# Low halves of the expert weights on one engine, one comparison for eight one-hot tiles, Silu and Tanh instead of Sigmoid

## The chip, the core and the metric

The kernel runs on one core of a Trainium2 chip. The metric is the device time of one execution in microseconds (us); the time given for a kernel is the median of its runs. Five engines work side by side and wait for each other through semaphores: PE (TensorE, matrix products; PEld are its weight loads), DVE (VectorE), ACT (ScalarE), POOL (GpSimd) and SP (SyncE, which here only issues transfers). Each engine works through its own list of instructions in order.

## The reference

One layer of a hybrid encoder over 1024 tokens of width 1024: four mixers side by side, an output projection, then a mixture of 16 experts and a gate. The change touches only the part behind the output projection:

```python
def expert_choice_moe(x, router_w, w_gate, w_up, w_down):
    aff = softmax(x @ router_w)                      # 1024 tokens x 16 experts
    gate, idx = top_k(swapaxes(aff), 128)            # each expert takes 128 tokens
    xs = x[idx]
    h = silu(xs @ w_gate) * (xs @ w_up)              # weights 1024 x 1024, fp32, per expert
    ye = (h @ w_down) * gate
    return zeros.at[idx].add(ye)

h = h + expert_choice_moe(rmsnorm(h, norm_ffn_w), ...)
gate = sigmoid(rmsnorm(h, ple_norm_w) @ ple_gate_w)
h = h + gate * (p @ ple_proj_w)
return rmsnorm(h, final_norm_w)
```

## The kernel before

The first 880 us hold the mixers and the output projection; the change does not touch them. After them `experts` walks through the 16 experts in turn. For each expert three matrices of 1024 x 1024 fp32 numbers are read from HBM, in tiles of 128 x 1024 (512 KB), 24 tiles an expert. `chunk` handles two tiles at a time: a transfer into a buffer `raw` (six of them; for early experts some go ahead of time into `room`), a cast on ACT into the high half `wh` (L1620), and a subtraction raw - wh that gives the low half `wl` (L1622). The subtraction frees the raw buffer, and SP then issues the next transfer into it. `mm3` multiplies in three passes: high x high (L1651), high x low (L1652), low x high (L1653). `up` does this for the gate and up matrices, `down` for the third one.

`spare` decides which engine subtracts. It counts the tiles: from the second expert's worth of tiles on, six of every 24 go to POOL, and from the tenth expert on four of every 24; all others go to DVE. Two tiles of the first expert go to POOL by an argument of their own.

Three more things belong to the change:

- `slot_sums` turns the slot numbers of an expert's tokens into one-hot matrices: eight comparisons of 128 x 128 on DVE (L1926), each followed by a small product (L1927). `pick` uses it for each of the 16 experts, `pick_tile` for each of seven groups of 128 finished tokens.
- `up` ends with silu: ACT computes a sigmoid (L1991), and DVE multiplies twice (L1992 by the gate product, L1993 by the up product).
- `tile_finish` computes the sigmoid gate of a group of finished tokens (from the 11th expert on, a group per expert): a sigmoid on ACT (L2164), a multiplication by the projected embedding `pp` (L2165), an addition (L2166). The group's rows come from HBM by indices, with transfers that POOL issues: `gather` (L1959) from `H` into `a` and from `PP` into `b`. Experts' tokens are gathered from `HN` two experts ahead, and their results are added to `H` by a scatter (L2012).

The instructions' order on each engine is worked out by a scheduler when the kernel is built, from what each one depends on; it is the same in every execution.

Of the kernel before, what the change touches and what calls it, by code (L numbers as in the profile page):

```python
# [25 lines left out]
def host_constants():  # L26
# [32 lines left out]
    # rotary tables  # L59
# [5 lines left out]
    # retention decays  # L65
# [8 lines left out]
    # long-filter features and decay  # L74
# [11 lines left out]
    # 2048-point transform as 16 x 128: cos, sin, -sin of [n2, k1 + 16 k2], and the same transposed  # L86
# [23 lines left out]
def woven(*parts):  # L110
    """emits the steps of several generators side by side, each spread over the whole"""
    work = [[list_len, g, 0] for g, list_len in parts]
    live = set(range(len(work)))
    while live:
        i = min(live, key=lambda k: (work[k][2] + 0.5) / work[k][0])
        try:
            next(work[i][1])
            work[i][2] += 1
            yield
        except StopIteration:  # L120
            live.discard(i)


class Body:
# [19 lines left out]
    @contextmanager  # L144
    def after(self, *ins):
        """what is traced here is queued behind these instructions"""
        with ExitStack() as order:
            for i in ins:
                if i is not None:
                    order.enter_context(self.tc.issue_after(i))  # L150
            yield
# [47 lines left out]
    def rsqrt(self, out, in_, scale, eps):  # L199
        """out = (in * scale + eps) ** -0.5"""  # L200
# [5 lines left out]
    def split_T(self, xn_tiles, half, w_name, hi, lo, tag, bufs):  # L206
        """transposes 4 token tiles [128, 1024] to hi/lo [128, 8, 512*half..], scaled per feature"""
# [55 lines left out]
    def load_w(self, w, segs):  # L263
        """columns of a weight [1024, n] -> (wh, wl) [128, 8, n], w == wh + wl"""
# [25 lines left out]
    def proj_cm(self, c0, evac):  # L290
        """128 channels of w_in, channel-major: evac(half, psum[128, 512]); 8 steps"""
# [15 lines left out]
    def proj_tm(self, segs, evac):  # L307
        """columns of w_in, token-major: evac(t, psum[128, n]); 16 steps"""
# [20 lines left out]
class Gdn:  # L329
    def conv_tile(self, c0, name, taps, ti, ntot, bias=None, half=True):  # L330
        """128 channels projected channel-major and convolved along time -> [128, 1024]"""
# [18 lines left out]
    def silu_half(self, out, acc):  # L350
        """out = silu(2 * acc)"""
# [5 lines left out]
    def softplus(self, out, x, n, tag):  # L357
        """out = log(1 + exp(x)) on [128, n], accurate to float32's rounding beside exp's own"""
# [17 lines left out]
    def bias_rows(self):  # L376
        """per-head constants on every partition"""
# [9 lines left out]
    def gdn_proj(self):  # L387
# [8 lines left out]
        # gates, token-major: z | a | b, and the state-space dt  # L396
# [44 lines left out]
    def swapped(self, ap, rev=False):  # L441
        """halves of each tile swapped, or all tokens of it reversed as well"""
        v = ap.rearrange("p (t b i) -> p t b i", t=8, b=2)
        return v[:, :, ::-1, ::-1] if rev else v[:, :, ::-1, :]
# [13 lines left out]
    def gdn_values(self):  # L458
        """4 steps"""
# [24 lines left out]
    def gdn_rates(self):  # L484
        nc = self.nc
        # [128, (kind dir head), tile]
# [8 lines left out]
        # rhs for the permuting products: g | beta | rk, as [dir, tile, head]  # L495
# [10 lines left out]
        # split of g for the decay sums  # L506
# [6 lines left out]
    def gdn_scalars(self):  # L513
# [10 lines left out]
        # e^{gc}, e^{gl - gc}, e^{gl} (other half), e^{gc} (own token order)  # L524
# [12 lines left out]
        # beta * rk of the column tokens, one row per block  # L537
# [11 lines left out]
    def gdn_prep(self, d, t):  # L549
        """decay, key and query products of one tile and direction; X to the block layout, the scan's matrices"""  # L550
# [42 lines left out]
        # decayed queries, in their own token order  # L593
# [10 lines left out]
        # decay of the state  # L604
# [4 lines left out]
        # token-major k in block order  # L609
# [12 lines left out]
    def gdn_inverse(self):  # L622
        """inverts the diagonal 32 x 32 blocks of every system, one system to a partition"""
        nc = self.nc
        # per row: first block | second block; the upper right blocks
# [3 lines left out]
        # per row: first inverse turned | first inverse | second inverse; products  # L629
# [30 lines left out]
    def gdn_scan(self):  # L660
# [11 lines left out]
        # rows of the upper token block: upper right block | inverse turned | inverse | its product; lower: 0 | inverse  # L672
# [13 lines left out]
        def place(d, s):  # L686
            """token half and state half of a step, and its block"""
# [17 lines left out]
        def invert(d, i, part):  # L705
            """the inverse's upper right block"""
# [17 lines left out]
        def solve(d, i):  # L724
            """the inverse times keys and values; values go under the states, keys into what multiplies the states"""
# [105 lines left out]
    def gdn_preps(self):  # L831
        """16 steps"""
# [8 lines left out]
# rows of a spectrum: k0, k8, then real and imaginary parts of these  # L841
# [7 lines left out]
class Mix:  # L849
    def tokens(self, src, fn, tag, bufs):  # L850
        """[128 channels, 1024 tokens] -> fn(tile slice, psum [128 tokens, 4 tiles, 128 channels])"""
# [8 lines left out]
    # ---- projections and convolutions -> DRAM  # L860
# [73 lines left out]
    # ---- state-space mixer  # L934
    def ssm(self):
# [7 lines left out]
        # a = dt * A, split; [128, dir, tile, head]  # L943
# [20 lines left out]
        def sc(x, t, n=64):  # L964
            """[128, 2, 32] scalars of a tile as [128, 4, 2, n]"""
            return x[:, :, t * 4:t * 4 + 4].rearrange("p d h -> p h d")[:, :, :, None].to_broadcast([128, 4, 2, n])

        # states before and after each tile, both directions; what a tile adds first stands in the next one's place
# [4 lines left out]
        # to what a tile adds, the state of the tile before comes, decayed over that tile  # L973
# [38 lines left out]
        def weights(t):  # L1012
            """decay from each source to each target"""
# [26 lines left out]
        def combine(t, E, pg, py, pi):  # L1040
            # forward and backward parts of the products of B and C, decayed
# [39 lines left out]
    def norm_store(self, y, t, col):  # L1081
        """rmsnorm over 256 columns, to the mixed rows; the norm's weights are in the rows of w_out"""
# [8 lines left out]
    # ---- long convolutions  # L1091
    def hy_mlp(self):
        """hidden layers of the filters' network: positions 512 h + c on the partitions of half h; and 1024 - (512 h + c)"""
# [44 lines left out]
    def hy_transforms(self):  # L1138
        """16-point parts of the transforms of filter and signal, 64 channels at a time -> DRAM; 8 + 8 steps"""
# [4 lines left out]
        # both directions of the filter as one circular one of 2048  # L1144
# [5 lines left out]
        for q in range(4):  # L1150
# [16 lines left out]
            # what passes straight through  # L1167
            nc.gpsimd.tensor_tensor(out=S[0:1, 0, 0], in0=S[0:1, 0, 0], in1=bi, op=OP.add)
            # sums and differences of points half a turn apart
# [16 lines left out]
    def spectrum(self, z, k1, M):  # L1186
        """the points k1 + 16 k2, real and imaginary"""
# [17 lines left out]
    def dft16(self, u, x, z, w):  # L1205
        """sums u and differences x [128, 8, n] of points n and n + 8 of 16 -> rows z(i), as above"""
# [45 lines left out]
    def idft16(self, z, y):  # L1252
        """transpose of dft16: z as above -> y [128, 8, 256]; even points first"""
# [64 lines left out]
    def hy(self):  # L1318
# [4 lines left out]
        def rows(name):  # L1323
            """row i of a spectrum, or n of them"""
# [18 lines left out]
        def forward(k1):  # L1343
# [5 lines left out]
            # product with the filter  # L1349
# [47 lines left out]
    # ---- retention  # L1397
    def ret(self):
        """8 steps for the states, 8 more for the outputs, tiles falling"""
# [8 lines left out]
        def pq2(rev):  # L1408
            """tail and head powers of each head, or head and tail, as [128, 4, 2, 64]"""
# [4 lines left out]
        # states before and after each tile, as in the state-space mixer  # L1414
# [6 lines left out]
        def decayed(d, t, src):  # L1421
            """adds the state of the tile before, decayed over that tile"""
# [49 lines left out]
        def finish(t, r, po):  # L1472
            # group norm over each head
# [10 lines left out]
            # in the place of the state it came from  # L1484
# [12 lines left out]
    def open_stage(self):  # L1497
        """long convolutions and state-space mixer where the projections were"""
# [10 lines left out]
    def open_spare(self):  # L1509
        """what the experts' phase has no room for"""  # L1510
# [30 lines left out]
    def projections(self):  # L1541
        """4 + 12 + 16 + 16 steps"""
# [35 lines left out]
class Ffn:  # L1578
    def pool(self, name, side):
        """a stack with one pool of its own"""  # L1580
# [21 lines left out]
    def chunk(self, w, c, pool=False, behind=(), norm=None, first=0, load_behind=None, load_on=None, raw=None, wh=None,  # L1602
              wl=None):
        """256 rows of a weight [1024, 1024], times a norm's weights -> [(hi, lo), (hi, lo)], [128, 1024] each"""
        nc = self.nc
        out = []
        for k in range(2):
# [6 lines left out]
            with self.after(*behind):  # L1614
# [4 lines left out]
                else:  # L1619
                    nc.scalar.copy(h, r)  # L1620
                    e = nc.gpsimd if pool or self.spare(self.turns) else nc.vector
# [4 lines left out]
    def spare(self, n):  # L1626
        """whether GpSimd takes the n-th conversion"""
        n -= 1
        return n >= 24 and n % 24 in ((3, 7, 11, 15, 19, 23) if n < 24 * FIRST else (0, 10, 17, 20))

    def rows_T(self, x, hi, lo, tag=("sp", 2), head=None):
        """[128 rows, 1024] -> transposed [128, 8, 128] split; the first columns may lie elsewhere"""
# [13 lines left out]
    def mm3(self, ps, xh, xl, k, w, half, first, last):  # L1646
        """three-pass product of one k tile into a 512-column half"""
# [7 lines left out]
    def sumsq_rstd(self, x, s):  # L1655
# [3 lines left out]
        self.on_pool = self.rsqrt(s[:, 1:2], s[:, 0:1], 1.0 / D, EPS)  # L1659

    def out_proj(self):
# [36 lines left out]
        def multiply(t, hi, lo, xt):  # L1698
            """a step before, between and after halves of the second half of the columns"""
# [14 lines left out]
        def route(t, xt):  # L1714
            """the norm's weights are in the router's, its scale comes with the softmax"""
# [11 lines left out]
            # softmax over the experts  # L1727
# [51 lines left out]
    def top_128(self, i, pt):  # L1779
        """takes the i-th tile's weights [16 experts, 128 tokens] into the search of each expert's 128 largest"""  # L1780
        nc = self.nc
        if i == 0:
            # lanes of 32 partitions, each a list of every expert
# [11 lines left out]
        def order(w):  # L1795
            """lists that rise, then fall, or the other way round: to falling ones"""
# [8 lines left out]
        def merge(w, x, out):  # L1805
            """the 128 largest of two falling lists, rising and falling"""
# [4 lines left out]
        # two tiles at a time, as four lists of 64  # L1811
# [32 lines left out]
    def slots_of(self):  # L1844
# [11 lines left out]
        # slots, counted from 1: larger ones first, then equal ones in order of tokens  # L1856
# [17 lines left out]
        # what a slot takes over: token within its tile, tile, gate in three parts  # L1874
# [17 lines left out]
    def ranks(self):  # L1892
        """tokens in order of the last expert that takes them, from 1; the last expert's own have none"""
# [26 lines left out]
    def slot_sums(self, slot, e, n):  # L1920
        """of what an expert's slots take over, n sums for each of the slots numbered from 1 [128, n]"""
# [322 lines left out]
```

## Time and profile before

| | |
|---|---|
| time, median of 3 runs | 1687.73 us (1683.22 to 1689.33) |
| span of the profiled execution | 1691.1 us (no other time of this execution is given) |
| PE busy | 1525.9 us, 90% |
| DVE busy | 1236.0 us, 73% |
| ACT busy | 863.1 us, 51% |
| POOL busy | 773.4 us, 46% |
| DMA | 362.55 MB, mean 214 GB/s |

The span runs from the first to the last instruction, and shares are of that span. Averages over the whole span mix the mixers with the experts, so the rows below are mostly cut by stretch: 880 to 960 us (the routing's end and the first expert), 960 to 1133 us (about four experts), 1133 to 1350 us (about five), 1350 to 1624 us (five, each with a gate group) and the rest. An instruction that waits inside an engine for a port or for operands counts as busy; an engine that waits for a semaphore counts as idle, and the profile says which instruction's end released it.

### The profile page before, as it was taken

Reading aid. Unit: us, or ns where it says so; the run is one execution under the profiler, and the core shown is the slowest. Engines: PE = TensorE matmul, PEld = TensorE weight load, DVE = VectorE, ACT = ScalarE, POOL = GpSimd, SP = SyncE. Lnnn points to the kernel's source line nnn. Section 1 sums busy time; section 2 is a strip of 40 time slices with the busy share of each in tenths; the row PEclk is TensorE's granted clock in tenths of the full one; section 3 lists DMA queues with packets and bytes.
Section 4 is the critical chain, followed back from the end, with each engine's and each line's share of the span. In section 5 each row is a group of like instructions: output and inputs, shape, how many; then the busy total and the mean of one; then the engine's idle time right before and its main releaser. Section 6 shows DMA issues by size and latency. Waiting matters only on the chain.

```text
span 1691.1 us, 26196 instructions
## 1 busy us (share of the span) xinstructions
PE 1525.9 (90%) x9148; PEld 1250.7 (74%) x9148; DVE 1236.0 (73%) x2175; ACT 863.1 (51%) x1413; POOL 773.4 (46%) x856
## 2 busy tenths in 40 slices
PE   4999998999999899689988988889888899889997
PEld 4877778998778767578876766677666688777786
DVE  5589777922546568756777998889888886877773
ACT  6254342133443345332335766677676667656762
POOL 3117665662763368451324344554444443344441
PEclk9999999998999899789989999999999999989998
DMA  5213557363553674263447987789999988877871
GB/s 181 56 37 111 155 175 234 110 182 112 146 145 115 238 236 134 72 203 133 178 149 280 351 318 268 272 301 345 337 335 331 319 292 288 295 274 253 287 276 51
DMA packets 200673, 362.55 MB, mean 214 GB/s; under 512 B 62046, under 2 KB 124732, under 8 KB 200285
## 3 DMA queue, kind: packets, MB, share of 16 engines
q1 hardware_dynamic: 169016, 296.13, 50.8%
q0 software_dynamic: 12400, 42.29, 8.2%
q10 hardware_dynamic: 19125, 22.45, 3.9%
q8 instruction: 72, 1.18, 0.3%
q14 instruction: 60, 0.49, 0.1%
HBM read 301.04 MB, written 59.77 MB: 213 GB/s over the span
## 4 chain that ended last, share of the span: by engine, by line
PE 41%; DVE 19%; DMA 18%; issue 10%; POOL 8%; ACT 5%; SPq 0%; POOLq 0%; ACTq 0%; DVEq 0%
PE pj L300 8%; DVE wl L1622 6%; PE pj L318 5%; PE ga L1652 4%; DMA raw<-in_exp_w_up_dram 4%; PE ga L1653 4%; PE ga L1651 4%; POOL prm L1208 2%; POOL prr L1208 2%; ACT wh L1620 2%; DMA a<-H,tidx 2%; DMA raw<-in_exp_w_gate_dram 2%; PE pj L1652 2%; PE pj L1653 2%; PE pj L1651 2%
## 5 line engine op out<-in xcount | busy, mean ns | idle before, releaser
L1622 DVE TENSOR_TENSOR wl<-raw,wh 128x1024 fp32r<-128x1024 f32 x270 | 388.2, 1464 | 75.1 <-ACT wh L1620 71.6
L1620 ACT CAST wh<-raw 128x1024 fp32r<-128x1024 f32 x344 | 356.4, 1053 | 145.8 <-DMA raw<-in_exp_w_gate_dram 50.2
L1622 POOL TENSOR_TENSOR wl<-raw,wh 128x1024 fp32r<-128x1024 f32 x74 | 195.4, 2642 | 230.8 <-ACT wh L1620 213.9
L1652 PE MATMUL ga<-wl,xh 128*128 128x512 f32 x512 | 210.1, 410 | 27.4 <-DVE wl L1622 15.0
L1653 PE MATMUL ga<-wh,xl 128*128 128x512 f32 x480 | 191.2, 399 | 0.0
L1651 PE MATMUL ga<-wh,xh 128*128 128x512 f32 x480 | 179.2, 409 | 3.6 <-ACT wh L1620 3.1
L1652 PEld LDWEIGHTS ga<-wl,xh 128*128 128x128 f32 x512 | 98.3, 192 | 63.6 <-DVE wl L1622 29.9
L300 PE MATMUL pj<-hnh,wh 128*128 128x512 f32 x288 | 120.1, 417 | 0.8 <-ACT cin L337 0.8
L318 PE MATMUL pj<-wh,hnh 128*128 128x256 f32 (+1 forms) x384 | 112.0, 292 | 9.5 <-DVE zss L915 6.9
L300 PE MATMUL pj<-hnl,wh 128*128 128x512 f32 x288 | 118.5, 411 | 0.0
L300 PE MATMUL pj<-hnh,wl 128*128 128x512 f32 x288 | 118.1, 410 | 0.0
L1652 PE MATMUL pj<-wl,hh 128*128 128x512 f32 x256 | 105.2, 412 | 11.7 <-DVE wl L1622 10.9
L1651 PEld LDWEIGHTS ga<-wh,xh 128*128 128x128 f32 x480 | 91.4, 193 | 26.8 <-ACT wh L1620 7.0
L318 PE MATMUL pj<-wh,hnl 128*128 128x256 f32 (+1 forms) x384 | 110.4, 288 | 0.0
L318 PE MATMUL pj<-wl,hnh 128*128 128x256 f32 (+1 forms) x384 | 110.4, 287 | 0.0
L1653 PEld LDWEIGHTS ga<-wh,xl 128*128 128x128 f32 x480 | 92.3, 192 | 17.0
L1653 PE MATMUL pj<-wh,hl 128*128 128x512 f32 x256 | 101.0, 399 | 0.0
L1651 PE MATMUL pj<-wh,hh 128*128 128x512 f32 x256 | 90.2, 401 | 1.3 <-ACT hh L1641 1.3
L318 PEld LDWEIGHTS pj<-wh,hnh 128*128 128x128 f32 x384 | 73.9, 193 | 11.8 <-issue 6.5
L346 DVE SCALAR_TENSOR_TENSOR cacc<-cin,pcolh,cacc 128x1024 f32<-128x1024 f32 x48 | 64.5, 1345 | 16.7 <-POOL prm L1208 6.9
L318 PEld LDWEIGHTS pj<-wh,hnl 128*128 128x128 f32 x384 | 74.0, 193 | 0.5 <-issue 0.3
L318 PEld LDWEIGHTS pj<-wl,hnh 128*128 128x128 f32 x384 | 73.9, 193 | 0.5 <-issue 0.3
(542 smaller groups left out, 3823.5 us busy)
## 6 DMA issues: line engine op xcount, KB each, us to landing
raw<-in_exp_w_down_dram SPq DMA_DIRECT2D x128, 512.0 KB, 5.6
raw<-in_exp_w_gate_dram SPq DMA_DIRECT2D x108, 512.0 KB, 5.4
raw<-in_exp_w_up_dram SPq DMA_DIRECT2D x104, 512.0 KB, 5.4
wraw<-in_w_in_dram SPq DMA_DIRECT2D x30, 512.0 KB, 3.7
g<-WD SPq DMA_DIRECT2D x16, 768.0 KB, 5.7
room<-in_exp_w_up_dram SPq DMA_DIRECT2D x24, 512.0 KB, 5.2
WD<-gB SPq DMA_DIRECT2D x16, 640.0 KB, 3.2
room<-in_exp_w_gate_dram SPq DMA_DIRECT2D x18, 512.0 KB, 5.6
```

The costliest lines, as they stand in the source:

```text
L300: self.on_pj = nc.tensor.matmul(pj, lhsT=A[:, kt], rhs=B[:, kt, hs], start=i == 0, stop=i == 23)
L318: self.on_pj = nc.tensor.matmul(pj, lhsT=A[:, kt, ts], rhs=B[:, kt, :], start=i == 0, stop=i == 23)
L346: nc.vector.scalar_tensor_tensor(acc, cin[:, 2 - r + j:2 - r + j + 1024], w[j], acc, op0=OP.mult, op1=OP.add)
L1208: tt = lambda o, a, b, op: nc.gpsimd.tensor_tensor(out=o, in0=a, in1=b, op=op)
L1620: nc.scalar.copy(h, r)
L1622: e.tensor_tensor(out=l, in0=r, in1=h.bitcast(F32), op=OP.subtract)
L1651: nc.tensor.matmul(ps, lhsT=xh[:, k], rhs=wh[:, hs], start=first, stop=False)
L1652: nc.tensor.matmul(ps, lhsT=xh[:, k], rhs=wl[:, hs], start=False, stop=False)
L1653: return nc.tensor.matmul(ps, lhsT=xl[:, k], rhs=wh[:, hs], start=False, stop=last)
```

## The change

All subtractions of an expert's weights go to DVE, except the two that the first expert gives to POOL by argument: the function `spare` is gone. In the built programs POOL has 84 subtractions of line L1622 before and 6 in the change, so 78 move to DVE. The eight comparisons of a one-hot set become one instruction over 128 x 1024 elements, with both operands broadcast; the eight products follow it. There are 23 sets. Silu on ACT replaces sigmoid and one of the two multiplications. In the gate, sigmoid(x) * pp is written as (tanh(x / 2) + 1) * (pp / 2): the factor 1/2 for x goes into the scale that comes from the norm, the one for pp into the copy that writes it, and the addition of 1 and the product are one DVE instruction.

```diff
     def chunk(...):
                 nc.scalar.copy(h, r)
-                e = nc.gpsimd if pool or self.spare(self.turns) else nc.vector
+                e = nc.gpsimd if pool else nc.vector
                 e.tensor_tensor(out=l, in0=r, in1=h.bitcast(F32), op=OP.subtract)
...
-    def spare(self, n):
-        n -= 1
-        return n >= 24 and n % 24 in ((3, 7, 11, 15, 19, 23) if n < 24 * FIRST else (0, 10, 17, 20))
...
-    def sumsq_rstd(self, x, s):
+    def sumsq_rstd(self, x, s, half=1):
...
-        self.on_pool = self.rsqrt(s[:, 1:2], s[:, 0:1], 1.0 / D, EPS)
+        self.on_pool = self.rsqrt(s[:, 1:2], s[:, 0:1], half * half / D, half * half * EPS)
...
     def slot_sums(self, slot, e, n):
+        nc.vector.tensor_tensor(out=oh, in0=self.slots[:, None, :].to_broadcast([128, 8, 128]),
+                                in1=slot[:, :, None].to_broadcast([128, 8, 128]), op=OP.is_equal)
         for t in range(8):
-            nc.vector.tensor_scalar(oh[:, t], self.slots, slot(t), None, op0=OP.is_equal)
             self.on_pe = nc.tensor.matmul(pi, lhsT=oh[:, t], rhs=self.aux[:, e, t, 0:n], start=t == 0, stop=t == 7)
...
     def up(self, e, hi, lo):
-            nc.scalar.activation(h[:, hs], ps[0][half], AF.Sigmoid)
-            nc.vector.tensor_tensor(out=h[:, hs], in0=ps[0][half], in1=h[:, hs], op=OP.mult)
+            nc.scalar.activation(h[:, hs], ps[0][half], AF.Silu)
             nc.vector.tensor_tensor(out=h[:, hs], in0=ps[1][half], in1=h[:, hs], op=OP.mult)
...
     def ple_proj(self, wh, wl, tiles):
-                on_act = nc.scalar.copy(o, ps)
+                on_act = nc.scalar.activation(o, ps, AF.Copy, scale=0.5)
...
     def tile_turn(self, h, pp, idx, tag="h"):
-            self.sumsq_rstd(h, s)
+            self.sumsq_rstd(h, s, 2)
...
     def tile_finish(self, h, pp, idx, s, hi, lo, last=False):
-            nc.scalar.activation(sg, ps, AF.Sigmoid, scale=s[:, 1:2])
-            nc.vector.tensor_tensor(out=sg, in0=sg, in1=pp[:, hs], op=OP.mult)
+            nc.scalar.activation(sg, ps, AF.Tanh, scale=s[:, 1:2])
+            nc.vector.scalar_tensor_tensor(sg, sg, 1.0, pp[:, hs], op0=OP.add, op1=OP.mult)
             nc.vector.tensor_tensor(out=h[:, hs], in0=sg, in1=h[:, hs], op=OP.add)
```

Two places show what the scheduler makes of it. The first is POOL's list around the third to fifth expert, before; `a` are gathers, `H` scatters, `wl` low halves.

```order
L1959 DMA a_9694<-HN,pidx 128x1024
L1622 TENSOR_TENSOR wl_9610<-raw,wh_9609 128x1024
L1959 DMA a_10088<-HN,pidx 128x1024
L1622 TENSOR_TENSOR wl_9658<-raw,wh_9657 128x1024
L2012 DMA H<-b_9674,pidx 1024x1024
L1622 TENSOR_TENSOR wl_9787<-raw,wh_9786 128x1024
L1622 TENSOR_TENSOR wl_9835<-raw,wh_9834 128x1024
L1622 TENSOR_TENSOR wl_9883<-room,wh_9882 128x1024
L1622 TENSOR_TENSOR wl_9931<-room,wh_9930 128x1024
L1622 TENSOR_TENSOR wl_10004<-raw,wh_10003 128x1024
L1959 DMA a_10452<-HN,pidx 128x1024
```

The same place on POOL in the change (the lines of the gather and the scatter are now L1956 and L2008).

```order
L1956 DMA a_9655<-HN,pidx 128x1024
L1956 DMA a_10040<-HN,pidx 128x1024
L2008 DMA H<-b_9635,pidx 1024x1024
L1956 DMA a_10395<-HN,pidx 128x1024
L2008 DMA H<-b_10020,pidx 1024x1024
L2008 DMA H<-b_10375,pidx 1024x1024
L1956 DMA a_10750<-HN,pidx 128x1024
```

All low halves have left POOL's list; gathers and scatters stand one behind the other.

The second place is DVE's list at the end of the third expert's `up`, before.

```order
L1992 TENSOR_TENSOR c_9947<-ga,c_9947 128x512 x2
L1622 TENSOR_TENSOR wl_10022<-raw,wh_10021 128x1024
L1993 TENSOR_TENSOR c_9947<-ga,c_9947 128x512
L1622 TENSOR_TENSOR wl_10028<-raw,wh_10027 128x1024
L1993 TENSOR_TENSOR c_9947<-tk,c_9947 128x512
L1642 TENSOR_TENSOR xl<-sp,xh 128x512 x2
L1940 COPY pg<-sp 128x5
L1926 TENSOR_SCALAR oh<-slots,slot 128x128 x3
L1932 SCALAR_TENSOR_TENSOR pg<-pg 128x1
L1942 TENSOR_TENSOR pg<-pg 128x1
L1926 TENSOR_SCALAR oh<-slots,slot 128x128 x3
L1622 TENSOR_TENSOR wl_10046<-raw,wh_10045 128x1024
```

The same place in the change.

```order
L1989 TENSOR_TENSOR c_9901<-ga,c_9901 128x512
L1989 TENSOR_TENSOR c_9901<-tk,c_9901 128x512
L1622 TENSOR_TENSOR wl_9974<-raw,wh_9973 128x1024
L1637 TENSOR_TENSOR xl<-sp,xh 128x512 x2
L1622 TENSOR_TENSOR wl_9980<-raw,wh_9979 128x1024
L1937 COPY pg<-sp 128x5
L1921 TENSOR_TENSOR oh<-slots,slot 128x1024
L1929 SCALAR_TENSOR_TENSOR pg<-pg 128x1
L1939 TENSOR_TENSOR pg<-pg 128x1
```

Two of the four multiplications into `c` are gone, the one-hot set is one row of 128 x 1024, and the low halves stand where they stood, with POOL's share among them. ACT's list has eight table loads before and eight in the change; the last one stands ahead of the first L1988 (Silu), and none stands between Silu and Tanh later on. The transfers on SP keep their order but for four that move by a place or two.

## Rows read from the trace of the kernel before

**Rows 1.** The page: span and number of instructions.

```profile
span 1691.1 us, 26196 instructions
```

**Rows 2.** Busy time by stretch: start:end, length, engines, granted clock, DMA share, GB/s.

```profile
core 0: us, PE busy (x) PEld busy (x) DVE busy (x) ACT busy (x) POOL busy (x), PEclk, DMA share, GB/s
880.00:960.00 80.00, 71.91 (x376) 57.05 (x374) 69.00 (x157) 53.03 (x73) 33.96 (x19) 0.96 0.81 298
960.00:1133.00 173.00, 151.46 (x694) 116.49 (x693) 156.89 (x164) 113.46 (x130) 83.78 (x34) 0.98 0.82 291
1133.00:1350.00 217.00, 192.66 (x857) 143.29 (x856) 183.56 (x225) 150.21 (x168) 99.09 (x42) 0.98 0.93 333
1350.00:1624.00 274.00, 254.64 (x1408) 214.56 (x1407) 210.24 (x282) 179.23 (x247) 111.48 (x66) 0.98 0.83 287
```

**Rows 3.** Waits of PE, 960 to 1133 us: total, times, longest.

```profile
PE ga L1652 <- DVE wl L1622: 8.4, 6, 2.3
PE pj L1652 <- DVE wl L1622: 6.2, 5, 1.7
PE ga L1652 <- POOL wl L1622: 5.1, 3, 3.0
```

**Rows 4.** Waits of PE, 1133 to 1350 us.

```profile
PE ga L1652 <- DVE wl L1622: 5.4, 8, 1.7
PE ga L1652 <- POOL wl L1622: 5.0, 8, 1.7
PE pj L1652 <- DVE wl L1622: 4.7, 8, 1.1
```

**Rows 5.** Waits of PE, 1350 to 1624 us.

```profile
PE sp L1640 <- DMA a<-H,tidx: 10.7, 3, 7.7
```

**Rows 6.** Busy time of line L1622 alone, by stretch: DVE, POOL.

```profile
960.00:1133.00 173.00, 124.43 (x74) 65.98 (x25) 0.98 0.82 291
1133.00:1350.00 217.00, 131.77 (x88) 79.49 (x29) 0.98 0.93 333
880.00:1691.00 811.00, 436.47 (x304) 214.09 (x80) 0.98 0.81 287
```

**Rows 7.** Timeline, 921 to 936 us: start, length, engine, line.

```profile
922.05 11.43 DVE L1622 TENSOR_TENSOR wl<-room,wh 128x1024 fp32r<-128x1024 f32 x10
922.81 12.65 POOL L1959 DMA_INDIRECT a<-HN,pidx  x1 [8.35 <-PE ga L1653]
```

**Rows 8.** Timeline, 1031 to 1042 us.

```profile
1030.00 11.48 DVE L1622 TENSOR_TENSOR wl<-raw,wh 128x1024 fp32r<-128x1024 f32 x5 [2.76 <-ACT wh L1620]
1032.96 2.94 POOL L1622 TENSOR_TENSOR wl<-raw,wh 128x1024 fp32r<-128x1024 f32 x1
1037.05 0.50 PE L1652 MATMUL ga<-wl,xh 128*128 128x512 f32 x1 [1.03 <-DVE wl L1622]
```

**Rows 9.** Busy time of line L1926 alone.

```profile
880.00:1691.00 811.00, 57.46 (x184) 0.98 0.81 287
```

**Rows 10.** Groups by line: busy us, mean ns, idle before.

```profile
L1992 DVE TENSOR_TENSOR c<-ga,c 128x512 f32<-128x512 f32 x32 | 20.8, 682 | 3.5 <-ACT c L1991 3.4
L1991 ACT ACTIVATE c<-ga 128x512 f32<-128x512 f32 x32 | 17.7, 594 | 2.2 <-PE ga L1653 2.1
L354 ACT ACTIVATE cth<-cacc 128x1024 f32<-128x1024 f32 x12 | 12.7, 1058 | 20.8 <-DVE cacc L346 11.5 <-DMA gB<-in_hy_filt_b_mid_dram 6.2 <-PE tk L455 3.0
L1618 DVE SCALAR_TENSOR_TENSOR gl<-raw,pcol,gh 128x1024 fp32r<-128x1024 f32 x8 | 9.9, 1271 | 0.0
```

**Rows 11.** Timeline, 1488 to 1512 us.

```profile
1489.13 4.10 DVE L1926 TENSOR_SCALAR oh<-slots,rk 128x128 bf16<-128x128 bf16 x7
1494.59 6.89 DVE L1622 TENSOR_TENSOR wl<-raw,wh 128x1024 fp32r<-128x1024 f32 x6
1495.33 7.01 POOL L1959 DMA_INDIRECT a<-H,tidx  x1 [2.80 <-DMA out_dram<-a,tidx]
```

**Rows 12.** Line L1959, count and ns minimum/median/maximum.

```profile
L1959 POOL DMA_INDIRECT a<-H,tidx x7: 954/1799/7006, 1334.5 to 1621.5; - x7
```

More of the change, by code (lines that the diff above doesn't have):

```diff
@@ L1939, in pick @@
         idx = self.t6([128, 1], "pidx", 6, dt=I32)
-        nc.vector.tensor_copy(g[:, 0:5], self.slot_sums(lambda t: self.slot[:, t, e:e + 1], e, 5))
+        nc.vector.tensor_copy(g[:, 0:5], self.slot_sums(self.slot[:, :, e], e, 5))
         self.picked = self.token_index(g, idx)
@@ L1952, in pick_tile @@
         idx = self.t6([128, 1], "tidx", 3, dt=I32)
-        nc.vector.tensor_copy(g[:, 0:2], self.slot_sums(lambda t: r[:, t:t + 1], 0, 2))
+        nc.vector.tensor_copy(g[:, 0:2], self.slot_sums(r, 0, 2))
         self.token_index(g, idx)
```

## The prediction

> **What bounds the kernel now.** The span [rows 1] is cut into stretches first [rows 2], because everything the change touches lies behind 880 us. There PE is busy for 151.5 of 173 us, 192.7 of 217 and 254.6 of 274: it idles 21.5, 24.3 and 19.4 us. That idle time, with about 8 us of the first stretch, is what a change off PE can win. The other columns say what could stand behind it. DVE is busy 156.9 of 173 us (91%) in the second stretch, 183.6 of 217 (85%) in the third and 77% in the fourth; the transfers take 82%, 93% and 83% of their engines' time. So the second stretch belongs to PE and DVE, the third to PE, DVE and the transfers together, the fourth mostly to PE.
>
> PE's waits agree. In the second stretch PE waits 8.4 + 6.2 us for low halves made by DVE and 5.1 us for those made by POOL [rows 3], 19.7 of its 21.5 us idle. In the third it is 5.4 + 4.7 + 5.0 = 15.1 us of 24.3 [rows 4]. In the fourth the largest wait is another one: 10.7 us in three waits for the gathered rows of finished tokens [rows 5].
>
> Why do low halves come late? Ten subtractions that stand back to back on DVE take 11.43 us, 1.143 us each [rows 7]. Five others take 11.48 us, where 5.7 would do [rows 8]: POOL's own subtraction of 2.94 us starts inside them, and PE then waits 1.03 us for the low half. So the two engines shut each other out: the offloaded tile takes longer on POOL than on DVE, and stops DVE too. Over all of 880 to 1691 us, 304 subtractions keep DVE busy 436.5 us [rows 6]; at 1.143 they would need 347.5. Some 89 us of DVE's busy time are waits of this kind.
>
> **The change part by part.**
>
> *78 subtractions move to DVE.* 78 x 1.143 = 89.2 us more work, 89 us less shutting out: DVE's total for this line stays where it is (382 x 1.143 = 436.6 against 436.5). By stretch it does not cancel: in the second, 74 x 1.143 = 84.6 of 124.4 us is work, so 39.8 go, and 25 x 1.143 = 28.6 come: -11.2. In the third 131.8 - 100.6 = 31.2 go and 29 x 1.143 = 33.1 come: +2. What falls besides is the delay of the moved tile, from 65.98 / 25 = 2.6 us on POOL to 1.14 on DVE. The duration of a subtraction without POOL beside it is known [rows 7], so its only unknown is whether some other POOL work still shuts DVE out; nothing is left in POOL's list there but gathers, scatters and small work on norms, and ten subtractions ran at full pace beside a gather [rows 7]. Bounds: from nothing left of the 89 us, to a tenth of it.
>
> *One comparison for eight.* 184 comparisons keep DVE busy 57.5 us [rows 9], 2.5 us a set; at 1489 us seven of a set took 4.10 us by themselves [rows 11]. The broadcast comparison of 128 x 1024 does not occur before. The nearest row is the subtraction of the same size, 1.14; the upper bound is what a set costs now, 2.5. I take 1.14, since it too is one pass over 1024 elements with two inputs: 23 x 1.14 = 26, a gain of 31 us of DVE time (0 to 31). The first of the eight products now waits for the whole set instead of an eighth of it. PE works in order, so if it comes there early, the expert's matrix products queued behind stand still for up to 1.14 - 0.14 = 1 us, 23 us over all sets. I take nothing of it, since a set of eight ends no later than before and the last product has always waited for all eight; the 23 us stay in the range. The picked indices themselves are wanted two experts later, and for the groups of finished tokens the gather may come 1 us later, seven times, at worst 7 us in a stretch where PE waits for it.
>
> *Silu.* 32 multiplications of 682 ns (20.8 us in all [rows 10]) leave DVE. Silu itself does not occur before; Sigmoid takes 594 ns on the same shape, and Tanh over twice the width 1058 [rows 10], as much for an element. The same duration for all three is taken, with ACT idle for 59.5 us of the second stretch and 66.8 of the third as cover [rows 2]. A function that needs another table would show a load in ACT's list; there is none more than before.
>
> *Tanh in the gate.* A scalar_tensor_tensor takes the place of a tensor_tensor 32 times. Where both run over 1024 elements they take 1271 ns [rows 10] and 1143: for a quarter of the width at most 0.1 us each, up to 3 us on DVE in a stretch in which it idles 64 us. I take nothing. The factor 1/2 in 16 copies of the first stretch costs ACT at most 0.1 us each, 0 to 2 us, with ACT idle 27 us there.
>
> *The sum.* DVE: 0 - 31 - 21 = about 50 us less of the 619.7 of the four stretches [rows 2]. The second stretch falls from 156.9 to about 135 of 173 us (-11 here, -5 for eight multiplications, -5 for four sets); it no longer bounds it. PE gets at most 21.5 us back there. I take two thirds, 14: what is left is late transfers, at 82% of their engines' time. In the third, DVE loses about 14 us (+2, -7 for ten multiplications, -9 for seven sets), PE waits 15.1 us for low halves, and the transfers can go from 93% to 100%, 7% or 15 us. I take half of 15, 8. In the fourth the wait for gathered rows stays, and of the 8.7 us beside it I take 4. The first stretch gives 1, its comparisons. Together 27: from the span of 1691.1 us to 1664. The median of the runs is 1687.7, 0.2% below that span, so the forecast is 1661. From below the gain is bounded by the case that only the second stretch gains, 5 us; from above by 21.5 + 15 + 8.7 = 45.
>
> **The rivals.**
>
> *GpSimd's issue of gathers starves: slower.* POOL's issue of one gather took 12.65 us beside ten subtractions [rows 7]; beside six others the gather of finished rows took 7.01 us [rows 11], of a shortest 0.95 and a median 1.8 [rows 12], and it is this gather that PE waits for [rows 5]. In the change DVE's list has four to six more subtractions an expert and fewer gaps. If each of the seven gathers of finished tokens took 7.0 instead of 1.8 us and PE waited for all of it, 7 x 5.2 = 36 us come on top: 1661 + 36 = 1697. It decides from 27 / 7 = 3.9 us a gather on. Against it: POOL no longer has its own subtractions ahead of a gather, and DVE idles 64 us in that stretch and will idle more, and each gap lets POOL in. By the Trainium skill ("SBUF — State Buffer", section "SBUF: two separate sides", on DMAs issued by GpSimd) descriptors are locked out while VectorE runs a two-port instruction, and a subtraction of two tensors is not one, so this rival would be nil and the forecast would stand at 1661, against 1697 by the longest rows. The 12.65 us [rows 7] disagree with that rule, and the measurement decides.
>
> *The transfers hold: no change.* If the transfers' 93% of the third stretch is their limit already and the second follows them as soon as DVE is out of the way, only some 5 us of the second stretch remain: 1683. For it: 333 GB/s is the highest rate of the four stretches. Against it: the second stretch reads at 291 GB/s, so it has room.
>
> *All waits for low halves go.* 21.5 + 15 + 8: 1643. For it: DVE falls to 78% in the second stretch. Against it: a tile still has a transfer, a cast and a subtraction in line, each able to be late.
>
> **How the numbers follow.** The forecast, 1661 with its own range 1650 to 1673, gets 0.60; all waits gone 0.13, transfers hold 0.15, starved gathers 0.12. A difference of 0.5% is 8.4 us and about what a measurement of this kernel can tell from none. Faster by more than that is then 0.60 + 0.13 = 0.73, within it 0.15, slower 0.12. The range for 8 in 10 leaves out the starved gathers and the tail below 1640: 1638 to 1688.
>
> **What would show it.** In the profile of the change POOL's line L1622 has 6 instructions, and DVE's 382 lie between 1.2 and 1.25 us with hardly a longer one; a mean over 1.3 would prove the first step wrong. DVE's busy time behind 880 us is about 50 us less. A one-hot set takes 1.1 to 1.3 us; 2.5 would cost the 31 us. PE's waits for low halves fall from 35 us in the second and third stretch to under 15. The transfers of the third stretch run above 333 GB/s. The forecast fails if gathers of `H` take 5 us or more on POOL and PE waits behind them, or if PE's waits for low halves stay with the transfers, not DVE, as what came last.

## The result and the profile after

The changed kernel takes 1662.21 us (median of 4 runs, 1658.55 to 1665.13) against 1688.53 us before: a ratio of 0.984, with a 95% interval of 0.9818 to 0.9863. The forecast was 1661. The profiled execution has a span of 1663.3 us, where the sum said 1664. The total came out as worked out; the stretches that it came from did not.

The stretches are cut at the same places of the program as in [rows 2], the Silu (before, the Sigmoid) of the 2nd, 6th, 11th and 16th expert. The first view gives the busy time of the engines of the changed kernel in them.

```profile
880.00:960.00 80.00, 71.79 (x372) 57.66 (x371) 66.55 (x115) 52.57 (x73) 19.29 (x18) 0.94 0.81 299
960.00:1108.00 148.00, 145.11 (x696) 115.77 (x695) 133.76 (x151) 112.55 (x129) 22.66 (x8) 1.00 0.94 340
1108.00:1321.00 213.00, 189.35 (x850) 144.04 (x849) 175.17 (x195) 150.29 (x167) 26.84 (x13) 0.98 0.96 340
1321.00:1599.00 278.00, 260.56 (x1423) 222.00 (x1422) 207.75 (x252) 180.59 (x248) 48.04 (x44) 0.96 0.83 286
```

The second stretch took 173 us and takes 148. PE idled 21.5 us in it and idles 2.9; its busy time fell too, from 151.5 to 145.1 us, with a granted clock of 1.00 instead of 0.98. The third fell from 217 to 213 us, the fourth rose from 274 to 278, and what lies behind fell from 67 to 64. So the second stretch alone, experts 3 to 6, holds 25 of the 28 us. It now moves 340 GB/s instead of 291, with the transfers busy 94%; the third moves 340 instead of 333, at 96%. PE's waits for low halves in the second stretch were 19.7 us [rows 3] and are now 1.0:

```profile
PE pj L1647 <- DVE wl L1622: 0.5, 2, 0.4
PE ga L1647 <- DVE wl L1622: 0.5, 1, 0.5
```

The low halves that DVE makes from `raw`, before and after: busy us, mean ns, idle before.

```profile
L1622 DVE TENSOR_TENSOR wl<-raw,wh 128x1024 fp32r<-128x1024 f32 x270 | 388.2, 1464 | 75.1 <-ACT wh L1620 71.6 <-PE ga L1653 2.2 <-PE tk L1652 0.2
L1622 DVE TENSOR_TENSOR wl<-raw,wh 128x1024 fp32r<-128x1024 f32 x340 | 407.8, 1221 | 79.4 <-ACT wh L1620 74.6
```

The mean fell from 1.46 us to 1.22. With those from `room`, DVE has 78 more of them than before, and the longest takes 1.76 us instead of 4.10. PE's waits for low halves in the third stretch, beside the largest wait there:

```profile
PE ga L1646 <- ACT wh L1620: 12.4, 7, 2.9
PE ga L1647 <- DVE wl L1622: 4.3, 10, 0.5
PE pj L1647 <- DVE wl L1622: 3.6, 6, 0.7
```

In [rows 4] it was 15.1 us for low halves in waits of up to 1.7 us. They fell to 7.9 us, none over 0.7, but PE now waits 12.4 us for high halves, which ACT makes directly behind a transfer. The wait moved one step up the chain, and PE idles 23.7 us of this stretch where it idled 24.3. In the fourth stretch one wait stands out:

```profile
PE sp L1635 <- DMA a<-H,tidx: 17.1, 4, 5.8
```

That wait stood at 10.7 us [rows 5] and is now longer. Yet PE's idle time as a whole did not grow: it is 17.4 us of 278, where it was 19.4 of 274. What grew is PE's busy time, from 254.6 to 260.6 us, with a granted clock of 0.96 instead of 0.98. The trace shows the two side by side. At 1471 us PE waits 5.8 us for a gather, and the 10 us with that wait and the 10 us behind it read, with the columns of [rows 2]:

```profile
1470.00:1480.00 10.00, 4.21 (x17) 3.50 (x16) 4.60 (x5) 4.26 (x6) 0.30 (x1) 0.82 0.91 360
1480.00:1490.00 10.00, 10.00 (x56) 8.71 (x56) 7.38 (x9) 7.34 (x12) 0.75 (x2) 0.84 0.40 130
```

For a part of each, the granted clock was at the lower of its two levels, 1.2 instead of 2.4 GHz. So a wait of PE costs more here than its own length. By the clocks of the whole stretch that is 2% of some 255 us, about 5 us; this is an estimate from the two rows.

It is not that POOL's issue of these gathers starves, as the counts of line L1956 (count, ns minimum/median/maximum) show:

```profile
L1956 POOL DMA_INDIRECT a<-H,tidx x7: 977/1032/2277, 1308.5 to 1589.9; - x7
```

The longest issue was 7.0 us before [rows 12] and is 2.3 now. The gather itself starts late, for a reason that the section on the fourth stretch shows.

### The profile page after: what moved, and what is told of

It is laid out like the page before. It is cut to its first block, busy times and chain, and to the rows that moved or that the text cites. A ratio compares the mean times of both kernels' runs of the same rounds, so it can differ in the third digit from the quotient of the medians.

```text
span 1663.3 us, 25974 instructions
## 1 busy us (share of the span) xinstructions
PE 1523.9 (92%) x9148; PEld 1262.2 (76%) x9148; DVE 1197.4 (72%) x2060; ACT 863.1 (52%) x1413; POOL 557.0 (33%) x778
## 4 chain that ended last, share of the span: by engine, by line
PE 56%; DMA 17%; DVE 12%; POOL 6%; issue 5%; ACT 4%; SPq 0%; POOLq 0%; ACTq 0%; DVEq 0%
PE pj L300 9%; PE ga L1648 6%; PE ga L1647 5%; PE ga L1646 5%; PE pj L318 5%; DMA raw<-in_exp_w_gate_dram 4%; DMA raw<-in_exp_w_up_dram 3%; PE pj L1647 3%; PE pj L1646 3%; DVE wl L1622 3%; PE pj L1648 3%; DMA a<-H,tidx 2%; POOL prm L1208 2%; POOL prr L1208 2%; PE sp L1635 2%
## 5 line engine op out<-in xcount | busy, mean ns | idle before, releaser
L1622 DVE TENSOR_TENSOR wl<-raw,wh 128x1024 fp32r<-128x1024 f32 x340 | 407.8, 1221 | 79.4 <-ACT wh L1620 74.6
L1646 PE MATMUL ga<-wh,xh 128*128 128x512 f32 x480 | 177.7, 409 | 13.7 <-ACT wh L1620 13.3
L2008 POOL DMA_INDIRECT H<-b,pidx x15 | 37.0, 2467 | 249.1 <-ACT b L2007 143.4
L1956 POOL DMA_INDIRECT a<-HN,pidx x16 | 31.0, 1940 | 207.0 <-PE pj L1647 67.7
```

The source lines that it names most:

```text
L1622: e.tensor_tensor(out=l, in0=r, in1=h.bitcast(F32), op=OP.subtract)
L1646: nc.tensor.matmul(ps, lhsT=xh[:, k], rhs=wh[:, hs], start=first, stop=False)
L1956: self.fetched = self.nc.gpsimd.indirect_dma_start(out=xg, out_offset=None, in_=self.HN if src is None else src, in_offset=bass.IndirectOf ...
L2008: nc.gpsimd.indirect_dma_start(out=self.H, out_offset=bass.IndirectOffsetOnAxis(ap=idx[:, :1], axis=0), in_=y, in_offset=None, compute_op= ...
```

## The experiments

Each run is compared with runs of the kernel before on the same chip, whose medians lie between 1687.2 and 1689.2 us. Ratios are to those runs, with their 95% interval.

**Which part gives the time?** Three kernels apply one part each to the kernel before. The first:

```diff
-                    e = nc.gpsimd if pool or self.spare(self.turns) else nc.vector
+                    e = nc.gpsimd if pool else nc.vector
```

> The kernel before with the low halves alone moved to DVE; comparisons, Sigmoid and the gate as before. Theory A (the two engines shut each other out, and a low half from POOL comes late): most of the 26 us, 1670 us, and no subtraction on DVE over 1.3 us. Theory B (DVE was short of time, and what it is relieved of is the comparisons and multiplications, some 50 us of work): DVE's total for subtractions is the same as before, so 1685 us, no change.

It took 1659.4 us (five runs, 1655 to 1668), a ratio of 0.9812 (0.9783 to 0.984): all of the gain, and 11 us more than theory A's number. The comparisons left as they were show, in the groups of DVE in this kernel, what else happened:

```profile
L1926 DVE TENSOR_SCALAR oh<-slots,slot 128x128 bf16<-128x128 bf16 x128 | 23.8, 266 | 0.0
L1926 DVE TENSOR_SCALAR oh<-slots,rk 128x128 bf16<-128x128 bf16 x56 | 10.2, 257 | 0.0
```

All 184 comparisons now take 34 us where they took 57.5 [rows 9], without being touched. Before, ten of them took over 1.3 us, up to 3.13, each with a subtraction of POOL's under way; here none does. POOL's subtractions had shut them out too.

The second part alone:

```diff
+        nc.vector.tensor_tensor(out=oh, in0=self.slots[:, None, :].to_broadcast([128, 8, 128]),
+                                in1=slot[:, :, None].to_broadcast([128, 8, 128]), op=OP.is_equal)
         for t in range(8):
-            nc.vector.tensor_scalar(oh[:, t], self.slots, slot(t), None, op0=OP.is_equal)
```

> The kernel before with the broadcast comparison alone. A set falls from 2.5 us of DVE time to 1.21, 30 us in all. Theory A: the comparisons matter little beside the subtractions, -4 us, 1684. Theory B: 31 of 50 us of DVE's relief, -15 us, 1673.

It took 1675.2 us, 0.9923 (0.9896 to 0.9951), close to theory B's number. But the theory fails on the other two. The groups of DVE in this kernel, with POOL still subtracting:

```profile
L1925 DVE TENSOR_TENSOR oh<-slots,slot 128x1024 bf16<-128x1024 bf16 x16 | 22.3, 1394 | 0.0
L1925 DVE TENSOR_TENSOR oh<-slots,rk 128x1024 bf16<-128x1024 bf16 x7 | 8.5, 1211 | 0.0
```

Two of the 23 are stretched, to 1.96 and 3.36 us, where ten of the 184 small ones were: 30.8 us in all instead of 57.5.

The third part alone:

```diff
-            nc.scalar.activation(h[:, hs], ps[0][half], AF.Sigmoid)
-            nc.vector.tensor_tensor(out=h[:, hs], in0=ps[0][half], in1=h[:, hs], op=OP.mult)
+            nc.scalar.activation(h[:, hs], ps[0][half], AF.Silu)
```

with Tanh in the gate.

> The kernel before with Silu and Tanh alone. 32 multiplications of 0.68 us leave DVE, 21 us. Theory A: -3 us, 1685. Theory B: 21 of 50 us of relief, -10 us, 1678.

It took 1687.5 us (ten runs), 0.9994 (0.998 to 1.0008): nothing, although 21 us of work left DVE. So theory B, that DVE's load counts as such, falls here and with the first kernel.

The reverse of the second kernel, the changed kernel with the eight comparisons put back:

```diff
-        nc.vector.tensor_tensor(out=oh, in0=self.slots[:, None, :].to_broadcast([128, 8, 128]),
-                                in1=slot[:, :, None].to_broadcast([128, 8, 128]), op=OP.is_equal)
         for t in range(8):
+            nc.vector.tensor_scalar(oh[:, t], self.slots, slot(t), None, op0=OP.is_equal)
```

> The changed kernel with the eight single comparisons put back. If comparisons cost time only because POOL's subtractions shut them out, nothing is lost here: 1662 us. If the single comparison saves time of its own, as it does in the kernel before, 1670 us or more.

It took 1664.4 us, 0.9863 (0.9837 to 0.9888), the same as the changed kernel within what the intervals tell. The comparison wins some 12 us where POOL subtracts and nothing that can be told in the changed kernel, where it does not. In part, two parts of the change remove the same loss: 23 of the 57.5 us. That is not all of it, since behind another order of the gathers (below) the same comparison is worth 8 us without any subtraction of POOL's beside it.

**Do the two engines stop each other, or is it that POOL's low halves come late?** In the changed kernel POOL gets back subtractions at the places where it had them, but nobody reads what they write.

```diff
                     e.tensor_tensor(out=l, in0=r, in1=h.bitcast(F32), op=OP.subtract)
+                    if self.turns <= 24 * FIRST and self.spare(self.turns):
+                        idle = self.t3([128, 1024], "junk", 1, dt=BF16)
+                        nc.gpsimd.tensor_tensor(out=idle, in0=h.bitcast(F32), in1=h.bitcast(F32), op=OP.subtract)
```

> The changed kernel, and POOL runs 54 more subtractions (first nine experts behind the first, at the places where it had them before) whose result nobody reads; DVE still makes every low half and its list of instructions is the changed kernel's. Shutting out by the shared port: DVE's subtractions stretch again, some to over 3 us, and with all of its own work on top DVE is worse off than before in 960 to 1133 us: 1680 us or more. If only the late low halves from POOL had cost the time, nothing on the path waits for POOL here: 1662 us.

It took 1707.8 us, 1.01 (1.0066 to 1.0134): slower than the kernel before, and 46 us slower than the changed one. The timeline of this kernel shows how:

```profile
1034.10 5.19 DVE L1622 TENSOR_TENSOR wl<-raw,wh 128x1024 fp32r<-128x1024 f32 x3 [2.06 <-ACT wh L1620]
1034.21 2.87 POOL L1625 TENSOR_TENSOR junk<-wh 128x1024 bf16<-128x1024 f32 x1 [6.65 <-ACT wh L1620]
1038.49 2.56 POOL L1625 TENSOR_TENSOR junk<-wh 128x1024 bf16<-128x1024 f32 x1 [1.41 <-ACT wh L1620]
1039.22 10.29 DVE L1622 TENSOR_TENSOR wl<-room,wh 128x1024 fp32r<-128x1024 f32 x6
```

Three subtractions of DVE take 5.19 us instead of 3.4, six take 10.29 instead of 6.9, with subtractions of POOL's under way in both. Over the whole kernel the same 382 subtractions keep DVE busy 522.4 us, where it was 455.7. In 960 to 1133 us DVE is now busy almost throughout (first engine PE, third DVE):

```profile
960.00:1133.00 173.00, 151.94 (x690) 112.76 (x689) 168.24 (x150) 112.72 (x128) 69.42 (x33) 1.00 0.86 294
```

168.2 of 173 us, with DVE's list of instructions that of the changed kernel, where 133.8 of 148 do. No low half of POOL's is waited for, and yet the time is lost. POOL's extra instruction reads the high half and could hold that buffer longer, but the trace names no instruction that waited for it. What this run does not show is that the lateness of POOL's own low halves cost nothing: PE's 5.1 and 5.0 us of waits for them [rows 3, 4] were part of the loss before.

The Trainium skill ("SBUF — State Buffer", section "Who interferes with whom") calls the ports that VectorE and GpSimd share an exclusive lock, which an instruction holds from start to end. This trace agrees in kind: six subtractions take 10.29 us with POOL's beside them, where 6.9 would do.

**Why did the third stretch gain 4 us and not 8?** Two kernels read only half of each weight tile of five experts, one built on the changed kernel, one on the kernel before.

```diff
-                (load_on or nc.sync).dma_start(r, w[c * 256 + k * 128:c * 256 + k * 128 + 128])
+                rows = w[c * 256 + k * 128:c * 256 + k * 128 + 128]
+                if half:
+                    (load_on or nc.sync).dma_start(r[:, 0:512], rows[:, 0:512])
+                    r = r[:, None, 0:512].to_broadcast([128, 2, 512])
+                else:
+                    (load_on or nc.sync).dma_start(r, rows)
```

> The changed kernel, reading only half of each weight tile of five experts (gate and up of the 7th to 11th expert, down of the 6th to 10th; the cast and the subtraction run over the half twice, at full size), so part of the weights is left out. If the transfers set the time from 1108 to 1321 us, PE gets most of its 24 us idle back there: 1645 us or less. If DVE, ACT or PE's own order sets it, no change: 1662.

> The same halved transfers in the kernel before. If the transfers held 1133 to 1350 us there as well, the gain is as large as in the changed kernel, some 17 us: 1670. If POOL's and DVE's shutting out held it, under 5 us: 1683 or more.

On the changed kernel: 1647.7 us, 0.9755 (0.9733 to 0.9778), 14.5 us less. On the kernel before: 1681.6 us, 0.9965 (0.9949 to 0.998), 6.5 us less, between the two expectations. The same stretch of the program, first in the changed kernel with half the reads:

```profile
1109.00:1304.00 195.00, 181.51 (x855) 145.18 (x854) 178.53 (x202) 150.32 (x174) 34.17 (x13) 0.97 0.73 220
```

And in the kernel before with half the reads:

```profile
1127.00:1337.00 210.00, 186.50 (x845) 144.93 (x844) 204.26 (x229) 149.40 (x170) 109.61 (x42) 0.97 0.68 205
```

With the transfers relieved, the changed kernel walks through in 195 us instead of 213. Not all of it is kept: the fourth stretch takes 285 us in that kernel instead of 278, and PE's waits for gathered rows there grow to 24.3 us. The kernel before needs 210 instead of 217, since DVE is then busy 204.3 of 210 us and PE waits 20.0 us for its low halves. So the third stretch of the kernel before had two limits close to each other, DVE with POOL beside it and the transfers, and the change removed the first of them only.

**Why did the fourth stretch lose?** Cut at the same places, the profiles of the other kernels show which part lengthens it: 268 us with only the low halves moved, 277 with Silu and Tanh added (the kernel with the eight comparisons put back), 278 with all three. These are profiles of one execution each; by them the stretch shrinks with the first part (from 274) and grows again when the third is added. PE waits there for the gathers of finished rows. Gathers of expert tokens (from `HN`) and of finished rows (from `H`) share two buffers, and they alternate, so that a gather of finished rows goes into the buffer of the group before, which is free only when that group's result has been written. POOL's list in the changed kernel shows such a write, and the gather that was released when it had landed:

```profile
1354.24 1.76 POOL L2168 DMA_INDIRECT out_dram<-a,tidx  x1 [1.61 <-DVE a L2167]
1362.03 2.28 POOL L1956 DMA_INDIRECT a<-H,tidx  x1 [6.03 <-DMA out_dram<-a,tidx]
```

The experiment changes the order of the two for every second group, so that it goes into the buffer of tokens that have just been turned.

```diff
+            own = self.gather(ti[i], self.H) if i >= 0 and i % 2 else None
             if e + 2 < NE:
                 xg.append(self.gather(pk[e + 2][0]))
...
-                tile = self.tile_start(ti[i])
+                tile = self.tile_start(ti[i], own)
```

> The changed kernel, gathering every second group of finished rows into the buffer of the expert tokens just used and not into that of the group before, so that three of its gathers no longer stand behind the write of the result. If these gathers set the time from 1321 to 1599 us, where PE waits 17 us for them, some 8 us go: 1654. If those waits are cover for something else that is as late, 1662.

It took 1654.8 us, 0.9801 (0.9773 to 0.9829), as expected. Then for the four groups that allow it (`if i > 0`), on the changed kernel and on the kernel before with only the low halves moved:

> The changed kernel with the gathers of four groups of finished rows (2nd to 5th) into the buffer of the expert tokens just used. The crossing of every second group cut PE's waits for these gathers from 17 to 12 us and the time to 1655; with all four crossed PE's waits for them fall to some 5 us: 1650 us. If PE then waits for something else that is as late, 1655.

> The kernel before with the low halves alone on DVE, and the same four gathers crossed; eight comparisons, Sigmoid and two multiplications as before. If the single comparison and Silu are worth nothing once POOL no longer subtracts, it is as fast as the one above, 1650 us; if they give DVE room that the crossing needs, 1658.

The first took 1641.6 us, 0.9724 (0.9707 to 0.9741): faster than both kernels, 21 us below the changed one. The waits of PE in its fourth stretch:

```profile
PE sp L1635 <- DMA a<-H,tidx: 3.0, 2, 2.3
```

The busy times there, with the columns of [rows 2]:

```profile
1316.00:1574.00 258.00, 253.44 (x1424) 215.66 (x1423) 206.88 (x252) 179.19 (x247) 45.47 (x44) 0.99 0.90 308
```

The fourth stretch takes 258 us instead of 278. PE's idle time there fell by 13 us to 4.6, and its busy time by 7 us to 253.4, with the granted clock at 0.99. The second kernel, though, took 1663.2 us, 0.9848 (0.9832 to 0.9864): no gain over only_low, and above both numbers expected, so the other two parts are not worth nothing here. Two more kernels put one of them back each into the crossed kernel.

> The changed kernel with all four gathers crossed and the eight single comparisons put back. With Sigmoid and eight comparisons the crossing came to 1663 us, with Silu and the single comparison to 1642. If the single comparison is what makes the difference (indices earlier, or less DVE time), this one is near 1663 us; if Silu and Tanh make it, near 1642.

> The changed kernel with all four gathers crossed, and Sigmoid with its second multiplication and the plain gate put back. If the single comparison makes the difference, near 1642 us; if Silu and Tanh make it, near 1663. If both are near 1642, only the two together cost, as where DVE's time runs short.

With eight comparisons it took 1650.0 us, 0.9779 (0.9763 to 0.9796), with Sigmoid 1654.8 us (1648 to 1661), 0.9805 (0.9768 to 0.9842). Neither number was expected: each part is worth something, 8 and 13 us over 1641.6, and 22 us together. PE's waits for gathers of finished rows behind 880 us give a reading, though not a full one. With both parts and no crossing they are 19.6 us, with only the low halves moved 15.4; with the crossing 5.9 and 13.7. So it seems that without the crossing what the two parts win ends in a longer wait for the gathers, and that with it it is kept. But the crossed kernels with one part put back have waits of 8.9 us (eight comparisons) and 6.0 us (Sigmoid): the second takes 13 us more than the crossed kernel at the same waits, so these waits do not explain what Silu is worth there. That, and why the crossing alone leaves 13.7 us of waits, is not settled; no run took it apart.

## Why the prediction was right, and where it was off

- *What bounds the kernel.* Right in kind for the second stretch: PE and DVE, with the two engines shutting each other out. pool_beside shows that this costs time without any low half of POOL's. Wrong in one step: PE's idle time was taken as all that a change off PE can win. The second stretch fell by 25 us, of which 18.6 were idle time and 6.4 busy time of PE. The clock is some 3 us of that (2% of 151 us, an estimate from the two rows). For the rest no run gives a reason; pool_beside has 151.9 us busy there at a clock of 1.00, so busy time of PE is not work alone.
- *78 subtractions move to DVE at no cost in its busy time.* 455.7 us for 382 in the changed kernel (1.193 each), against 436.6 by the sum: 19 us too low. The pace of 1.143 holds back to back alone; one that waits for ACT first takes 1.22. What it freed was right: their mean duration fell by some 0.25 us, and none is stretched by a subtraction of POOL's.
- *One comparison.* 1.21 us a set against 1.14, 27.9 us in all against 26. The gain of 31 us of DVE time was double counted: 23 of it is what the move of the subtractions gives by itself (57.5 to 34 us in only_low). In time it is some 12 us alone and nothing that can be told behind the first part. The wait of the products for the whole set cost nothing that can be seen.
- *Silu and Tanh.* The same durations as Sigmoid, 592 and 475 ns in the changed kernel. In time they give nothing as the kernel stands. That the gathers behind take it back is argued from their longer waits, not shown.
- *The sum.* Second stretch: -14 by the sum, -25 measured. DVE's 133.8 us there are the 135 that were forecast, but the two thirds of PE's idle time were too low: the transfers rose to 94%, and PE lost nearly all of it, and busy time besides. Third: -8 by the sum, -4 measured; PE's waits for low halves halved, but waits for high halves behind the transfers took their place. Fourth: -4 by the sum, +4 measured: the wait for gathered rows did not stay, it grew from 10.7 to 17.1 us; PE's idle time still fell by 2 us, but its busy time grew by 6 at the lower clock, which the sum leaves out. Errors of +11, -4 and -8 cancelled, with the ends of the kernel for the rest. That 1661 met 1662 is luck; that POOL's subtractions were the loss is not, as only_low and pool_beside show.
- *The rivals.* The starved gathers did not come: the longest issue of a gather of finished rows is 2.3 us, and it met two subtractions of DVE back to back, not six. The waits for gathers did grow, but behind the write that frees their buffer: in crossed_all, where four of the gathers no longer stand behind it, they are 3.0 us in the fourth stretch. The transfers hold, in the third stretch, as half_after shows; in the second they had the room that was read there. DVE is 38.7 us less busy behind 880 us (654.3 to 615.6), not 50.

## What to carry to other kernels

Work moved to a second engine is not free if the two engines stop each other: compare the mean of an operation with its best pace, and where it is a fifth longer, look at what the other engine does in that moment. Two parts of a change that remove the same loss do not add up, and what one part gives can depend on what stands behind it; test each alone and each taken away. Cut both kernels at the same places of the program before believing a total: here errors in three stretches cancelled. A gain that is read from a wait is certain only as far as what is late next, and here that was a transfer in one stretch and a buffer in another.

## What was not expected of the hardware

54 subtractions of 2.4 us on POOL that nobody waits for, 129 us of busy time on an engine that is otherwise busy for 128 of the 783 us behind 880 us, cost 46 us of the kernel's time. And the exclusion has a direction for transfers: ten of DVE's subtractions ran at full pace beside POOL's issue of a gather, while that issue took 12.65 us [rows 7], of a shortest 0.95 [rows 12].
